# A decoder block whose feed-forward products are shared: the seven products of a saved multiplication kept in the accumulators' banks and multiplied one unit earlier, with landing tiles of half the size

## The chip, the cores and the metric

The kernel runs on one NeuronCore of a Trainium2 chip. What is compared is the device time of one execution in microseconds. PE is the matrix engine (TensorE), PEld its weight loads, DVE the vector engine, ACT the scalar engine, POOL GpSimd and SP the engine that issues most transfers. SBUF is the on-chip memory that the engines work from; PSUM is the small memory that PE writes sums to, eight banks of 128 x 512 fp32 each.

## The reference

One layer on 256 tokens of width 2048, all in fp32:

```
h = h + 0.5 * swiglu(rms_norm(h), ffn1_w_gate, ffn1_w_up, ffn1_w_down)     # D_FF = 5632
n = rms_norm(h); P = n @ w_in                                             # 5376 columns
h = h + concat(retention(P), sliding_window_attention(P)) @ w_out
h = h + memory_cross_attention(rms_norm(h), rms_norm(mem))                # 256 memory tokens
h = h + 0.5 * swiglu(rms_norm(h), ffn2_w_gate, ffn2_w_up, ffn2_w_down)
out = rms_norm(h)

swiglu(x, g, u, d) = (silu(x @ g) * (x @ u)) @ d
```

The two feed-forward networks (FFN 1 and FFN 2) hold about two thirds of the time. The change is in them.

## The kernel before

**Three matmuls for one.** PE multiplies in a rounded fp32 (fp32r). Each factor is split into a high part (ACT copies it, rounded) and a low part (DVE subtracts the high part), and `three` issues high x high, high x low and low x high into the same sum. A split of a weight piece of 128 x 1024 takes one ACT instruction (tile `wh`) and one DVE instruction (tile `wl`); both tiles have four buffers.

**Units and steps.** The products with weights are written as a list of units. A `Unit` is one block of 512 output columns for all 256 tokens; t = 0, 1 are the two halves of the tokens, and each has its own PSUM bank. A unit goes through blocks of 512 rows of the weight, each in two steps of 256 rows: a step is 2 token halves x 2 row blocks of 128 x 3 = 12 matmuls of 128 x 512. `run_stream` walks over all steps; before it writes step *at* it writes the splits up to step at + 3 (LOOKAHEAD) and the loads up to at + 8. What finishes a block, or moves it, hangs on a list of tasks: `later(d, f)` runs f when d steps more have been written. Loads land in tiles named `wf`, 1 MB each, five of them, issued on SP's queue.

**Twins.** In the FFNs two blocks of output columns f = 0, 1 (gate and up of one block, or two blocks of the down product) go together as a `Twin`. Of its four blocks of 512 rows three are plain steps: 3 x 2 x 2 = 12 of them. The fourth (`seven`) is a 2 x 2 by 2 x 2 block product (token halves x row halves, row halves x f) done with seven products in place of eight, in Winograd's form. A product is a step of 6 matmuls. Some products take sums of the left factor (`sums`, from `sums_of`: four ACT copies, four DVE additions, and a split on both engines) and differences of the weights (DVE, line 222). Before, four of the seven products go to banks of their own (`tmp`), DVE adds them into SBUF tiles (`first_sums`, `second_sums`) while the plain steps add up in the two `acc` tiles, and `parts` adds the two at the end of the Twin: 8 DVE additions of 128 x 512 and one ACT copy for each Twin. The products are written behind plain steps 2 to 8 of their own Twin.

An FFN is: gate and up of block 0 as two Units, Twins for blocks 1 to 3, two Twins of the down product, Twins for 4 to 7, two Twins down, Twins for 8 to 10, four Units down. I number the Twins of one FFN T0 to T13. `gate_done` (Silu on ACT) and `up_done` (DVE) take a finished pair, `cross` transposes it (DVE), writes it to DRAM (SP) and reads it back (POOL).

## Time and profile before

| | us |
|---|---|
| median of 3 runs (2145.35 to 2149.93) | 2148.33 |
| the profiled execution | 2148.38 |
| its span on the core | 2146.2 |
| PE busy in it | 2129.7 |
| DVE busy | 1664.5 |
| ACT busy | 1144.4 |

The profiled execution's own time is 2.2 us over its span, and 0.05 us from the median. FFN 1 lies between about 5 and 730 us of the span, the mixer and the cross attention up to about 1440 us, and FFN 2 behind that. In the tables of groups one row is the instructions of one line with the same tiles and shape: busy time, mean ns of one, and the time that the engine stood idle just before them. In rows in order of time the first number is the start in us, the second the duration. A matmul's duration runs to its modelled end; the next one starts earlier than that.

### The profile page before, as it was taken

What the parts mean: (1) busy time and instruction counts of PE and PEld (TensorE: products, weight loads), DVE (VectorE), ACT (ScalarE), POOL (GpSimd) and SP (SyncE); (2) the same over time, 40 slices, a digit from 0 to 9 for tenths busy, and PEclk for the clock granted to TensorE, in tenths of its full rate; (3) what the DMA queues carried; (4) which work ended last, traced back from release to release, by engine and by line L of the source; (5) the groups of instructions that cost most, each with busy time, mean ns of one, the idle gap of its engine ahead of it and who ended that gap; (6) DMA issues with size and microseconds to landing.
All of it is one profiled execution on the core that took longest, in us unless ns stands there. A gap on an engine that the chain in (4) does not pass through costs nothing.

```text
span 2146.2 us, 25612 instructions
## 1 busy us (share of the span) xinstructions
PE 2129.7 (99%) x9624; PEld 1764.9 (82%) x9624; DVE 1664.5 (78%) x1984; ACT 1144.4 (53%) x1395; POOL 159.1 (7%) x273
## 2 busy tenths in 40 slices
PE   9999999999999999999999999999999999999998
PEld 7888888888888878888788888888888888888886
DVE  6988888888885778787665555567988888888875
ACT  6555555555554554646455444455655455555554
POOL 0000100001001110101110110010100000000000
PEclk9999999999999999999999999999999999999999
DMA  7767676767657666666776766476876575656663
GB/s 295 238 205 253 233 239 224 246 218 253 230 202 255 216 225 207 204 208 221 251 249 214 241 218 206 156 245 235 250 269 225 178 249 203 233 200 228 205 227 141
DMA packets 138444, 482.50 MB, mean 225 GB/s; under 512 B 11984, under 2 KB 11984, under 8 KB 138192
## 3 DMA queue, kind: packets, MB, share of 16 engines
q1 hardware_dynamic: 125888, 447.26, 59.7%
q0 software_dynamic: 12288, 33.57, 6.7%
q8 instruction: 75, 1.23, 0.2%
q14 instruction: 49, 0.40, 0.1%
q10 hardware_dynamic: 144, 0.05, 0.0%
HBM read 445.17 MB, written 35.65 MB: 224 GB/s over the span
## 4 chain that ended last, share of the span: by engine, by line
PE 57%; DVE 2%; DMA 2%; issue 1%; ACT 0%; POOL 0%; POOLq 0%; ACTq 0%; DVEq 0%
PE acc L633 17%; PE acc L632 17%; PE acc L634 17%; DMA t4k<-box 2%; PE tmp L634 2%; PE tmp L632 2%; PE tmp L633 2%; DVE wl L79 1%; DVE h L647 0%; PE tmp L866 0%; POOL t4k L619 0%; DVE t4k L610 0%; PE tmp L847 0%; DVE blk L520 0%; DMA box<-t4k 0%
## 5 line engine op out<-in xcount | busy, mean ns | idle before, releaser
L74 ACT ACTIVATE wh<-wf 128x1024 fp32r<-128x1024 f32 (+1 forms) x861 | 905.9, 1056 | 884.5 <-PE acc L634 819.5
L79 DVE TENSOR_TENSOR wl<-wf,wh 128x1024 fp32r<-128x1024 f32 (+1 forms) x861 | 1037.9, 1215 | 373.4 <-ACT wh L74 357.6
L632 PE MATMUL acc<-wh,blk 128*128 128x512 f32 (+1 forms) x2832 | 1100.6, 389 | 1.2 <-ACT wh L74 1.2
L633 PE MATMUL acc<-wl,blk 128*128 128x512 f32 (+1 forms) x2832 | 1099.1, 388 | 1.1 <-DVE wl L79 1.0
L634 PE MATMUL acc<-wh,blk 128*128 128x512 f32 (+1 forms) x2832 | 1098.1, 388 | 0.0
L632 PEld LDWEIGHTS acc<-wh,blk 128*128 128x128 f32 x2832 | 533.0, 188 | 112.2 <-ACT wh L74 2.4
L633 PEld LDWEIGHTS acc<-wl,blk 128*128 128x128 f32 x2832 | 533.0, 188 | 109.0 <-DVE wl L79 1.9
L634 PEld LDWEIGHTS acc<-wh,blk 128*128 128x128 f32 x2832 | 532.9, 188 | 108.7
L619 POOL DMA_DIRECT2D t4k<-box x256 | 147.8, 584 | 1772.3 <-DMA box<-t4k 748.4
L222 DVE TENSOR_TENSOR wf<-wf,wf 128x1024 f32<-128x1024 f32 x84 | 102.6, 1222 | 1.9
L632 PE MATMUL tmp<-wh,blk 128*128 128x512 f32 x224 | 87.1, 389 | 0.0
L633 PE MATMUL tmp<-wl,blk 128*128 128x512 f32 x224 | 87.1, 389 | 0.0
L634 PE MATMUL tmp<-wh,blk 128*128 128x512 f32 x224 | 87.1, 389 | 0.0
L249 DVE TENSOR_TENSOR t2k<-t2k,acc 128x512 f32<-128x512 f32 x112 | 71.8, 683 | 9.5 <-PE acc L634 9.5
L249 DVE TENSOR_TENSOR t2k<-t2k,tmp 128x512 f32<-128x512 f32 x112 | 76.5, 684 | 1.9
L610 DVE STREAM_TRANSPOSE t4k<-t2k 128x512 f32<-128x512 f32 x96 | 63.0, 691 | 10.2 <-ACT t2k L74 10.0
L634 PEld LDWEIGHTS tmp<-wh,blk 128*128 128x128 f32 x224 | 42.0, 188 | 8.7
L632 PEld LDWEIGHTS tmp<-wh,blk 128*128 128x128 f32 x224 | 42.0, 188 | 8.7
L633 PEld LDWEIGHTS tmp<-wl,blk 128*128 128x128 f32 x224 | 42.0, 188 | 8.7
L79 DVE TENSOR_TENSOR blk<-t4k,blk 128x512 fp32r<-128x512 f32 (+2 forms) x72 | 44.1, 653 | 4.8 <-ACT blk L74 4.6
L74 ACT ACTIVATE blk<-t4k 128x512 fp32r<-128x512 f32 (+2 forms) x72 | 39.2, 596 | 7.5 <-DMA t4k<-box 7.5
L647 DVE TENSOR_TENSOR h<-h,t4k 128x512 f32<-128x512 f32 x40 | 25.8, 687 | 16.6 <-DMA t4k<-box 16.6
(149 smaller groups left out, 720.1 us busy)
## 6 DMA issues: line engine op xcount, KB each, us to landing
wf<-in_ffn_w_up SPq DMA_DIRECT2D x88, 1024.0 KB, 6.6
wf<-in_ffn_w_down SPq DMA_DIRECT2D x88, 1024.0 KB, 6.9
wf<-in_ffn_w_gate SPq DMA_DIRECT2D x87, 1024.0 KB, 6.9
box<-t4k SPq DMA_DIRECT2D x64, 512.0 KB, 3.3
t4k<-box POOLq DMA_DIRECT2D x256, 128.0 KB, 7.0
wf<-in_w_in_rqk SPq DMA_DIRECT2D x16, 1024.0 KB, 7.4
wf<-in_w_in_rvg SPq DMA_DIRECT2D x16, 1024.0 KB, 5.4
wf<-in_w_out SPq DMA_DIRECT2D x16, 1024.0 KB, 8.0
```

Of the source, the lines that this page charges most:

```text
L74: return nc.scalar.activation(dst, src, AF.Copy, **kw)
L79: nc.vector.tensor_tensor(lo, src, hi, ALU.subtract)
L222: nc.vector.tensor_tensor(src, p, q, ALU.subtract)
L249: nc.vector.tensor_tensor(out, a, b, ALU.add)
L610: nc.vector.transpose(z[:, t, :].rearrange("p (g q j) -> p q g j", g=4, q=4), squares_of(v))
L619: nc.gpsimd.dma_start(z[32 * g : 32 * g + 32].rearrange("p t (i n) -> p (t i) n", i=4), far[g])
L632: nc.tensor.matmul(o, ah, bh, start=start, stop=False)
L633: nc.tensor.matmul(o, ah, bl, start=False, stop=False)
L634: nc.tensor.matmul(o, al, bh, start=False, stop=stop)
L647: nc.vector.tensor_tensor(v, v, out[t], ALU.add)
```

## The change

1. The seven products accumulate in the four banks that hold the Twin's result. The banks are named (f, t). P1 goes to (0,0), P5 to (1,1), P6 to (0,1), P3 to (1,0). After P6 DVE adds the copy of P1 onto bank (0,1) there (`middle`), and P7 is accumulated on top of it. After P7 ACT copies bank (0,1), and DVE adds this copy to bank (1,1) and another sum to (1,0) (`spread`). P2 and P4 and the plain steps are accumulated behind that, and the finished sums are read from PSUM. For each Twin this is 4 ACT copies and 4 DVE additions.
2. All Twins but the first of each FFN are `ahead`: P1, P5, P6, P3, P7 stand between the plain steps of the preceding Twin, P7 behind its last one; P2 and P4 stand between their own plain steps. T0 has P1, P5, P6, P3, P2, P7 one after the other ahead of its first plain step.
3. For that two Twins' banks are open at once. Every other Twin (T0, T2, ... `spare`) takes four `tmp` tiles of one bank, the others the two `acc` tiles of two banks.
4. Landing tiles are 128 x 1024 (512 KB), ten of them. A load of a paired weight takes half of both column blocks: 256 runs of 2 KB, before 256 runs of 4 KB. The other loads have runs of 4 KB as before, 128 of them.

The matmuls are the same in number, shape and line of `three`, and outside the FFNs they stand in the same order.

```diff
-    def big(dt=F32):
-        return wpool.tile([P, 2, 1024], dt, tag="wf", name=nm("wf"), bufs=5)
+    def land(dt=F32):
+        return wpool.tile([P, 1024], dt, tag="wf", name=nm("wf"), bufs=LAND)
...
+        plan = {
+            P1: ((0, 0), (0, 0), (0, 0)),
+            P5: ((1, 0), (1, 1), 0),
+            P6: ((1, 0), (0, 1), 1),
+            P7: ((0, 0), (0, 1), 2),
+            P2: ((0, 1), (0, 0), (1, 0)),
+            P4: ((0, 1), (0, 1), (1, 1)),
+            P3: ((1, 1), (1, 0), 3),
+        }
...
+        def bank(self, f, t):
+            if self.spare:
+                if (f, t) not in self.acc:
+                    self.acc[f, t] = tmp_ps()
+                return self.acc[f, t]
+            if f not in self.acc:
+                self.acc[f] = ps_acc.tile([P, 2, 512], F32, tag="acc", name=nm("acc"))
+            return self.acc[f][:, t, :]
...
+            if last and kind in (P1, P5, P6, P7):
+                later(0, {P1: self.keep, P5: self.keep_other, P6: self.middle, P7: self.spread}[kind])
...
-        def first_sums(self):
-            self.u2 = self.add(t2k(), self.u1, self.products[5])
-            self.u3 = self.add(t2k(), self.u2, self.products[4])
-            self.u5 = self.add(t2k(), self.u3, self.products[3])
-
-        def second_sums(self):
-            self.u4 = self.add(self.u2, self.u2, self.products[3])
-
-        def parts(self, f):
-            xs = (self.u4, self.u5) if f else (self.u1, self.u3)
-            return [self.add(x, x, self.acc[f][:, t, :]) for t, x in enumerate(xs)]
+        def middle(self):
+            x = self.bank(0, 1)
+            self.add(x, self.u1, x)
+            self.u2 = self.copied(x)
+            self.add(self.p5, self.p5, self.u2)
+
+        def spread(self):
+            for x, y in ((self.copied(self.bank(0, 1)), self.bank(1, 1)), (self.p5, self.bank(1, 0))):
+                self.add(y, x, y)
...
+            if isinstance(u, Twin):
+                if not u.ahead:
+                    out += u.chunks((P1, P5, P6, P3, P2, P7))
+                chunks = u.chunks((P2, P4) if u.ahead else (P4,))
+            own, n = len(chunks), len(x)
+            if isinstance(after, Twin) and after.ahead:
+                chunks += after.chunks((P1, P5, P6, P3, P7))
+            space = len(chunks) if len(chunks) > own else 2 * own
+            for at, step in enumerate(x):
+                out.append(step)
+                for i, c in enumerate(chunks):
+                    place = (2 * i + 1) * n // (2 * space)
+                    if i < own:
+                        place = min(place, n - 4)
+                    if place == at:
+                        out.append(c)
...
+        twins.append(Twin(*args, ahead=bool(twins), spare=len(twins) % 2 == 0))
```

The order of the instructions changes at two kinds of places that matter below. The first is the start of T0, here in FFN 1. On PE, before, the last matmuls of the block-0 unit (`acc_220`) are followed by T0's first plain step (`acc_530`):

```order
L633 MATMUL acc_220<-wl_431,blk_399 128x512
L634 MATMUL acc_220<-wh_430,blk_399 128x512
L632 MATMUL acc_530<-wh_450,blk_135 128x512 [waits PE_49,Activation_49]
L633 MATMUL acc_530<-wl_451,blk_135 128x512
L634 MATMUL acc_530<-wh_450,blk_135 128x512
```

Now the unit is followed by P1 (`tmp_557`, here its end) and P5 (`tmp_570`), whose left factor `blk_554` is the split of the sums:

```order
L643 MATMUL tmp_557<-wl_464,blk_414 128x512
L643 MATMUL tmp_557<-wh_463,blk_414 128x512
L643 MATMUL tmp_570<-wh_489,blk_554 128x512 [waits Activation_49]
L643 MATMUL tmp_570<-wl_490,blk_554 128x512 [waits DVE_49]
L643 MATMUL tmp_570<-wh_489,blk_554 128x512 [waits DVE_49]
```

P5, the first product that takes sums, now stands 6 matmuls behind the unit's end; before, 72 matmuls (five plain steps and two products without sums) stood in between. On DVE, before, the same place reads so (`t2k_489` and `t2k_490` are the finished block, `blk_519` the sums, `blk_564` their low part):

```order
L695 SCALAR_TENSOR_TENSOR t2k_489<-acc_220,n_102,t2k_489 128x512 [waits PE_49,Pool_49]
L695 SCALAR_TENSOR_TENSOR t2k_490<-acc_220,n_102,t2k_490 128x512
L610 STREAM_TRANSPOSE t4k_515<-t2k_489 128x4x4x32 [waits DVE_49]
L610 STREAM_TRANSPOSE t4k_515<-t2k_490 128x4x4x32 [waits DVE_49]
L79 TENSOR_TENSOR wl_525<-wf_448,wh_524 128x1024 [waits DMAHW0_49,Activation_49]
L279 TENSOR_TENSOR blk_519<-blk_519 128x256 x2
L279 TENSOR_TENSOR blk_519<-blk_519 128x256 [waits DVE_49]
L79 TENSOR_TENSOR wl_549<-wf_493,wh_548 128x1024 [waits Activation_49]
L279 TENSOR_TENSOR blk_519<-blk_519 128x256 [waits DVE_49]
L79 TENSOR_TENSOR wl_572<-wf_448,wh_571 128x1024 [waits Activation_49]
L222 TENSOR_TENSOR wf_448<-wf_495,wf_448 128x2x2x256 [waits DMAHW2_49]
L79 TENSOR_TENSOR blk_564<-blk_519,blk_564 128x1024 [waits Activation_49]
```

and now (`blk_534` the sums, `blk_554` their low part):

```order
L696 SCALAR_TENSOR_TENSOR t2k_505<-acc_235,n_102,t2k_505 128x512 [waits PE_49,Pool_49]
L696 SCALAR_TENSOR_TENSOR t2k_506<-acc_235,n_102,t2k_506 128x512
L617 STREAM_TRANSPOSE t4k_530<-t2k_505 128x4x4x32 [waits DVE_49]
L617 STREAM_TRANSPOSE t4k_530<-t2k_506 128x4x4x32 [waits DVE_49]
L82 TENSOR_TENSOR wl_540<-wf_509,wh_539 128x1024 [waits Activation_49]
L291 TENSOR_TENSOR blk_534<-blk_534 128x256 x2
L291 TENSOR_TENSOR blk_534<-blk_534 128x256 [waits DVE_49]
L82 TENSOR_TENSOR wl_567<-wf_543,wh_566 128x1024 [waits DMAHW1_49,Activation_49]
L291 TENSOR_TENSOR blk_534<-blk_534 128x256 [waits DVE_49]
L236 TENSOR_TENSOR wf_543<-wf_543,wf_486 128x2x2x256 [waits DVE_49]
L82 TENSOR_TENSOR blk_554<-blk_534,blk_554 128x1024 [waits Activation_49]
L82 TENSOR_TENSOR wl_581<-wf_461,wh_580 128x1024 [waits PE_49,Activation_49]
```

The row is nearly the same; one split has gone from between the sums and their low part, and PE stands at a product of the sums where it stood at a plain step.

The second place is the hand-over from one Twin to the next on PE, here T4 to T5 of FFN 1. Before, T4's last matmuls (`acc_1870`) are followed by T5's first plain step into its own tile:

```order
L633 MATMUL acc_1870<-wl_2074,blk_1672 128x512
L634 MATMUL acc_1870<-wh_2073,blk_1672 128x512
L632 MATMUL acc_2159<-wh_2084,blk_135 128x512 [waits DVE_49,Activation_49]
L633 MATMUL acc_2159<-wl_2085,blk_135 128x512
L634 MATMUL acc_2159<-wh_2084,blk_135 128x512
```

Now T5's P7 (left factor `blk_554`) ends T4's unit, and T5's first plain step (`blk_150`) follows it into the same tile of two banks:

```order
L643 MATMUL acc_2107<-wh_2245,blk_554 128x512 [waits Activation_49]
L643 MATMUL acc_2107<-wl_2246,blk_554 128x512 [waits DVE_49]
L643 MATMUL acc_2107<-wh_2245,blk_554 128x512 x2
L643 MATMUL acc_2107<-wl_2246,blk_554 128x512
L643 MATMUL acc_2107<-wh_2245,blk_554 128x512
L643 MATMUL acc_2107<-wh_2257,blk_150 128x512 [waits Activation_49]
L643 MATMUL acc_2107<-wl_2258,blk_150 128x512 [waits DVE_49]
L643 MATMUL acc_2107<-wh_2257,blk_150 128x512 x2
L643 MATMUL acc_2107<-wl_2258,blk_150 128x512
```

The plain step starts with bank (0,0). Bank (0,1), which `spread` copies, is written by the plain step's second six matmuls; none of those carries a wait on ACT, and the step's first matmul does: there the wait for the copy stands, since both banks are one tile. Where the next Twin has `tmp` tiles of one bank each, the wait for the copy stands at the seventh matmul.

## The prediction

> **What bounds the kernel now.** First the page (shares of the engines), then the stretches of time in which the change works, then who waits for whom, then the rows in order of time at the two places where the order changes.

> ```profile
> span 2146.2 us, 25612 instructions
> PE 2129.7 (99%) x9624; PEld 1764.9 (82%) x9624; DVE 1664.5 (78%) x1984; ACT 1144.4 (53%) x1395; POOL 159.1 (7%) x273
> 65.00:700.00 635.00, 635.00 (x2803) 525.82 (x2802) 536.69 (x565) 347.20 (x368) 46.05 (x80) 1.00 0.69 232
> 1500.00:2130.00 630.00, 630.00 (x2780) 521.50 (x2779) 529.11 (x553) 336.78 (x356) 32.25 (x56) 1.00 0.65 220
> ```

> The first two lines are the page. The other two are stretches of the FFNs: length, then the busy time of PE, PEld, DVE, ACT, POOL, the granted clock, and the DMA share. PE is busy in 635.00 of 635.00 and in 630.00 of 630.00 us, at full clock. In the FFNs there is no wait that could be taken away, and any wait that is added is paid in full.

> ```profile
> 49.10 0.39 PE L632 MATMUL acc<-wh,blk 128*128 128x512 f32 x1
> ...
> 51.82 0.39 PE L632 MATMUL acc<-wh,blk 128*128 128x512 f32 x1
> ACT wh L74 <- PE acc L634: 819.5, 598, 5.6
> L249 DVE TENSOR_TENSOR t2k<-t2k,tmp 128x512 f32<-128x512 f32 x112 | 76.5, 684 | 1.9
> L74 ACT ACTIVATE t2k<-tmp 128x512 f32<-128x512 f32 x32 | 18.5, 579 | 0.0
> L74 ACT ACTIVATE wh<-wf 128x1024 fp32r<-128x1024 f32 x852 | 901.1, 1061 | 882.4 <-PE acc L634 819.5 <-PE tmp L634 31.8 <-issue 9.2
> ```

> From 49.10 to 51.82 PE does the twelve matmuls of one step: 2.72 us, 0.227 each, so a product of 6 takes 1.36. ACT waits 819.5 us for PE (a buffer for `wh` comes free). A DVE addition takes 0.68 us, a copy out of PSUM 0.58, a high part 1.06.

> **What costs nothing.** The matmuls are the same; PE's work stays. Twenty-eight Twins lose 4 additions each: 112 x 0.684 = 77 us of DVE, off the path, since PE is busy in all of both stretches. They gain 3 copies each: 84 x 0.579 = 49 us of ACT, against 819.5 us in which ACT waits for PE; if that cover were gone, all of it would be paid. Where products stand between plain steps, `middle` has four of these, 10.9 us, until P7 needs its bank, for an addition and a copy.

> ```profile
> wf<-in_ffn_w_up SPq DMA_DIRECT2D x88, 1024.0 KB, 6.6
> box<-t4k SPq DMA_DIRECT2D x64, 512.0 KB, 3.3
> 2.60 0.52 SPq L333 DMA_DIRECT2D wf<-in_ffn_w_up  x1
> ```

> Landing: 1024 KB in runs of 4 KB take 6.6 us, 512 KB in runs of 2 KB (the write of `box`) 3.3: the same for a byte, and the DMA share has room from 0.69. SP issues 863 transfers (counted in the new order) in place of 476, at about half a microsecond each some 430 us of the span, in order; a `box` write waits on SP behind fewer outstanding bytes than before. Ten half tiles less the four that a Twin holds leave the loads some six steps, over 13 us, ahead: nothing. If transfers came late, DVE's and ACT's splits would be the first to wait.

> **Term 1: the start of T0.** P5 and P6 and P3 need the sums 1.36 us after the block-0 unit ends. ACT's and DVE's rows of FFN 1, before:

> ```profile
> 46.45 0.16 DVE L570 TENSOR_SCALAR ms<-tmp 128x2 f32<-128x2 f32 x1 [0.70 <-PE tmp L568]
> 49.36 1.27 ACT L674 ACTIVATE t2k<-acc,n 128x512 f32<-128x512 f32 x2 [2.49 <-PE acc L634]
> 51.61 1.23 DVE L79 TENSOR_TENSOR wl<-wf,wh 128x1024 fp32r<-128x1024 f32 x1 [3.48 <-ACT wh L74]
> 52.75 1.40 DVE L695 SCALAR_TENSOR_TENSOR t2k<-acc,n,t2k 128x512 f32<-128x512 f32 x2
> ...
> 58.53 0.42 DVE L279 TENSOR_TENSOR blk<-blk 128x256 f32<-128x256 f32 x1
> 58.86 1.22 DVE L79 TENSOR_TENSOR wl<-wf,wh 128x1024 fp32r<-128x1024 f32 x1
> 60.00 1.22 DVE L222 TENSOR_TENSOR wf<-wf,wf 128x1024 f32<-128x1024 f32 x1
> 61.13 1.23 DVE L79 TENSOR_TENSOR blk<-blk,blk 128x1024 fp32r<-128x1024 f32 x1
> ```

> The finished block (L695) to the fourth sum takes 52.75 to 58.86, 6.11 us, for ten instructions that stand in the new order too: the sums wait behind the finished block, its transposes and two splits. Then comes one subtraction (1.14 from start to start) and the low part (1.23), beside which ACT makes the high part. The chain begins a little later: from 46.61 on, DVE and ACT take turns for P5 and P6 (subtraction 1.14, high part 1.06, low part 1.14, subtraction 1.14, high part 1.06, low part 1.14) and are done at 53.4, not 52.75. So the low part is there at 53.4 + 6.11 + 1.14 + 1.23 = 61.9. P1 ends at 51.82 + 1.36 = 53.18; two matmuls of P5 need only the high part. PE loses 61.9 - 53.18 - 0.45 = 8.3 us. Later P7 waits for ACT's copy, which stands behind two high parts: 0.3.

> ```profile
> 1482.15 1.41 DVE L695 SCALAR_TENSOR_TENSOR t2k<-acc,n,t2k 128x512 f32<-128x512 f32 x2 [0.70 <-PE acc L634]
> ...
> 1487.93 0.42 DVE L279 TENSOR_TENSOR blk<-blk 128x256 f32<-128x256 f32 x1
> ...
> 1490.54 1.22 DVE L79 TENSOR_TENSOR blk<-blk,blk 128x1024 fp32r<-128x1024 f32 x1
> ```

> In FFN 2 the block's end was waited for until 1482.15, so PE's next matmul could start at about 1481.95 and P1 would end at 1483.3. L695 to the fourth sum is 6.12 us (1482.15 to 1488.27), now with 0.35 ahead of it (the rest of a subtraction), and behind it a split, a subtraction and the low part: 1482.5 + 6.12 + 1.14 + 1.14 + 1.22 = 1492.1. Meanwhile five matmuls can go. Loss: 1492.1 - 1483.3 - 1.13 = 7.7. Then P7's copy stands behind three high parts: 1.2.

> ```profile
> 1043.99 0.39 PE L632 MATMUL acc<-wh,blk 128*128 128x512 f32 x1
> 1045.93 0.62 PE L568 MATMUL tmp<-ones,t2k 128*128 128x1 f32 x4 [1.55 <-DVE t2k L565]
> 1046.42 0.78 PE L633 MATMUL acc<-wl,blk 128*128 128x512 f32 x1
> ...
> 1049.90 0.40 PE L632 MATMUL acc<-wh,blk 128*128 128x512 f32 x1
> 1040.00:1060.00 20.00, 18.45 (x77) 14.92 (x76) 11.95 (x15) 7.83 (x9) 3.03 (x5) 0.91 0.81 259
> ```

> A pause has a price behind it. After 1.9 us without work the eight matmuls from 1046.42 to 1049.90 took 3.48 us in place of 1.81, and the granted clock of the stretch is 0.91: 1.7 us lost. T0's pause is longer, so I take 1.6 each; none is the least, twice that the most. Term 1: 8.3 + 0.3 + 1.6 = 10.2 and 7.7 + 1.2 + 1.6 = 10.5, together 20.7 (14 to 26).

> **Term 2: the hand-over.** Before, no such wait stood there, so its price is put together:

> ```profile
> 1269.39 0.39 PE L634 MATMUL acc<-wh,blk 128*128 128x512 f32 x1
> 1269.82 0.69 ACT L74 ACTIVATE blk<-acc,nmem 128x512 fp32r<-128x512 f32 x1 [1.61 <-PE acc L634]
> 7.23 0.63 ACT L74 ACTIVATE wh<-wf 128x512 fp32r<-128x512 f32 x1 [1.28 <-DMA wf<-in_ffn_w_gate]
> 7.45 0.28 PE L634 MATMUL acc<-wh,blk 128*128 128x256 f32 x1
> 7.91 0.38 PE L632 MATMUL acc<-wh,blk 128*128 128x256 f32 x1 [0.18 <-ACT wh L74]
> ```

> ACT starts 0.43 us after the start of the last matmul that it waits for; the copy takes 0.58; PE starts 0.05 after ACT's end (7.86, 7.91), and the matmul after a wait takes 0.10 longer (0.38, 0.28). 0.43 + 0.58 + 0.05 + 0.10 less the usual 0.23 is 0.93 us. It is paid where the next Twin has the two-bank tiles: T1, T3, ..., T13, seven in each FFN. At the other hand-overs six matmuls, 1.36 us, lie between P7 and the wait, against 0.83: nothing. In FFN 1 the finished blocks of T4 and T10 are scaled by ACT, so a copy (to 1.01 after the unit's last matmul), a high part (to 2.07) and then the copy (to 2.65) precede: PE goes on at 2.70 where it would at 1.59, 1.21 with the 0.10. Term 2: 12 x 0.93 + 2 x 1.21 = 13.6 (8 if only the copy's 0.58 counts, 17 at 1.21 each).

> **Sum**, against the profiled execution's 2148.38 (0.05 from the median): 2148.4 + 20.7 + 13.6 = 2182.7, so 2183. Bounds of the terms: 2148.4 + 22 = 2170 and 2148.4 + 43 = 2191.

> **Rivals.**
> *The hand-over is free.* If only the bank that ACT reads were kept from PE, bank (0,0)'s six matmuls would cover it: 2148.4 + 20.7 = 2169. Against: the order has the wait at the first of them. [...]
> *T0's sums are early.* ACT's and DVE's queues may have the sums ahead of the finished block after all, if the 3.48 us in which DVE stands idle ahead of it (row at 51.61) are used for them; then T0 costs little: 2148.4 + 13.6 = 2162. Against: the sums stand behind L695 in the order, and that waits for PE.
> *PE passes a waiting matmul.* Behind P5 and behind each hand-over stand matmuls that wait for nothing. If PE went on with these, both terms would vanish, and 2148.4 is left, with a few us either way from waits outside the FFNs such as that at 1043.99: 2145 to 2150, not slower. It decides if PE passes at all. Against: at 1043.99 PE stood 1.9 us at a matmul that waited for DVE, with plain matmuls right behind it. [...]
> *ACT is late everywhere.* If a high part of 1.06 us precedes the copy at all 26 hand-overs, the twelve others cost about half a microsecond each and the fourteen 0.3 to 1.1 more: about 2197.

> **Chances.** Forecast 0.68; free hand-over 0.10; early sums 0.07; PE passes 0.05; ACT late 0.10. The range 2161 to 2193 takes in the first three and leaves out 0.15. A measurement of this kernel tells about 0.2% (4 us) from no change. PE passing is shared between faster and the same, with 0.01 of the rest for each of them: faster 0.03, same 0.04, slower 0.93.

> **What would show it.** PE's busy time in 65 to 700 us falls short of the stretch by about 8 us, at about 0.9 for each wait of `acc` for ACT's t2k copy, every second Twin. At 53 and at 1483 us PE stands 6 to 7 us for `blk`, and the granted clock behind it drops. DVE is busy some 75 us less, ACT 50 us more. I am wrong if PE stands at other places, above all if splits wait for `wf`, or if T0's waits are under 4 us.

## The result: 1.75% slower, as forecast

The changed kernel takes 2185.15 us (median of 4 runs, 2182.87 to 2187.39), the kernel before 2147.27 beside it: ratio 1.0175, 95% interval 1.0158 to 1.0193. The prediction was 2183. The profiled execution took 2185.12 us, its span is 2183.3.

The page of the changed kernel, and the two stretches of the FFNs (length, then PE, PEld, DVE, ACT, POOL, granted clock, DMA share):

```profile
span 2183.3 us, 26696 instructions
PE 2141.8 (98%) x9624; PEld 1767.3 (81%) x9624; DVE 1592.0 (73%) x1872; ACT 1180.0 (54%) x1479; POOL 159.2 (7%) x273
65.00:700.00 635.00, 629.94 (x2764) 518.47 (x2763) 489.38 (x494) 355.92 (x398) 43.75 (x76) 1.00 0.71 229
1500.00:2130.00 630.00, 617.90 (x2702) 507.58 (x2701) 485.59 (x492) 350.02 (x387) 34.58 (x60) 0.99 0.68 221
```

PE's matmuls are as many as before, DVE is busy 72 us less, and PE no longer fills its stretches: it misses 5.1 us in the first and 12.1 in the second, which holds T0's stop of FFN 2 (1502 to 1509) while T0 of FFN 1 lies ahead of the first. Its waits say where (us in all, times, longest; the last row is the kernel before):

```profile
PE tmp L643 <- ACT blk L77: 14.4, 2, 7.8
PE acc L643 <- ACT t2k L77: 9.8, 14, 0.8
PE tmp L575 <- DVE t2k L572: 5.0, 2, 4.1
PE tmp L568 <- DVE t2k L565: 4.3, 3, 1.8
```

The first row is T0's wait for the sums, twice; the second is the hand-over, fourteen times; the third is two waits for norms, 4.1 us of it for that of FFN 2, which was not in the prediction.

A wait's price is more than the wait (in FFN 1 T0's wait of 7.78 us for the sums stands in a stretch that grew by 11.1), so the time is also counted from start to start. All kernels run the same 9624 matmuls; numbered by their start in the trace, the time between the starts of two numbers is what that stretch of work took. In us:

```
matmuls        0-234   234-320  320-2900  2900-6500  6500-6732  6732-6830  6830-9400
               start   T0 FFN1  rest FFN1  middle     norm FFN2  T0 FFN2    rest FFN2
before          50.5    19.5     584.8      772.4      53.4       22.2       582.5
changed         51.5    30.6     592.2      766.5      59.0       33.1       589.6
changed again   50.7    30.9     592.2      770.5      58.5       33.1       589.6
e1 sums early   51.1    26.5     592.2      765.6      54.3       29.9       589.6
e2 one bank     51.2    30.1     584.8      764.6      59.9       32.5       582.5
e3 both         51.6    26.7     587.0      765.3      57.2       25.5       584.1
e4 half tiles   50.5    19.5     584.9      769.6      53.9       22.2       582.5
e5 norm first   50.9    31.0     592.2      765.8      52.3       33.5       589.6
e7 no subtr.    50.7    22.7     592.2      767.6      58.8       24.2       589.6
e8 copy twice   50.5    30.9     596.8      766.4      54.6       33.1       593.6
e6 T0 spread    55.7    21.6     585.3      765.7      54.5       23.7       582.5
e9 again        50.4    28.2     584.8      764.7      52.3       22.4       582.5
e10 norm later  50.5    28.2     584.8      764.6      53.6       23.1       582.5
e11 T0 mended   53.4    23.4     584.8      765.9      52.4       22.4       582.5
```

(In e6, e9, e10 and e11 some of T0's products stand among the matmuls numbered before T0's column, so there the two columns belong together.) The tail is 50.5 to 50.7 in all. Changed less before: 1.0, 11.1, 7.4, -5.9, 5.6, 10.9 and 7.1, together 37.2 us. So T0 cost 22.0, the hand-overs 14.5, and two things outside the prediction, +5.6 at the norm of FFN 2 and -5.9 in the middle, cancelled in this execution; in a second profile of the same kernel the middle gave only 1.9.

T0 of FFN 1, in order of time:

```profile
53.99 0.39 PE L643 MATMUL tmp<-wh,blk 128*128 128x512 f32 x1
54.81 1.40 DVE L696 SCALAR_TENSOR_TENSOR t2k<-acc,n,t2k 128x512 f32<-128x512 f32 x2
...
60.59 0.42 DVE L291 TENSOR_TENSOR blk<-blk 128x256 f32<-128x256 f32 x1
60.93 1.22 DVE L236 TENSOR_TENSOR wf<-wf,wf 128x1024 f32<-128x1024 f32 x1
61.05 1.06 ACT L77 ACTIVATE blk<-blk 128x1024 fp32r<-128x1024 f32 x1 [3.92 <-DVE blk L291]
...
62.13 1.22 DVE L82 TENSOR_TENSOR blk<-blk,blk 128x1024 fp32r<-128x1024 f32 x1
...
62.16 0.79 PE L643 MATMUL tmp<-wh,blk 128*128 128x512 f32 x1 [7.78 <-ACT blk L77]
...
63.41 1.22 PE L643 MATMUL tmp<-wh,blk 128*128 128x512 f32 x2
...
50.00:70.00 20.00, 12.18 (x43) 9.05 (x42) 16.10 (x19) 10.67 (x15) 2.47 (x4) 0.74 0.58 160
```

PE's matmul at 53.99 is the last of P1. The finished block (L696) comes first on DVE, the fourth sum (L291) at 60.59, ACT's high part of the sums behind that, and PE goes on at 62.16, 8.17 us later in place of 0.23. The low part (L82) is done at 63.35, and P5's third matmul, the first that needs it, starts at 63.41. The granted clock of these 20 us is 0.74: of the matmuls behind the stop eight start 0.43 us apart. In FFN 2 the like stop ends at 1509.26, 6.96 us behind P1's last matmul. At a hand-over into two-bank tiles:

```profile
112.74 0.39 PE L643 MATMUL acc<-wh,blk 128*128 128x512 f32 x1
113.16 0.60 ACT L77 ACTIVATE t2k<-acc 128x512 f32<-128x512 f32 x1 [0.30 <-PE acc L643]
...
113.81 0.50 PE L643 MATMUL acc<-wh,blk 128*128 128x512 f32 x1 [0.69 <-ACT t2k L77]
...
114.15 0.40 PE L643 MATMUL acc<-wl,blk 128*128 128x512 f32 x1
```

From 112.74 to 113.81 are 1.07 us, and 0.34 to the next, where 0.227 is usual: 0.96 us lost.

### The profile page after: what moved, and what is told of

Read it like the earlier page. It is cut to its first block, busy times and chain, and to the rows that moved or that the text cites. A ratio compares the mean times of both kernels' runs of the same rounds, so it can differ in the third digit from the quotient of the medians.

```text
span 2183.3 us, 26696 instructions
## 1 busy us (share of the span) xinstructions
PE 2141.8 (98%) x9624; PEld 1767.3 (81%) x9624; DVE 1592.0 (73%) x1872; ACT 1180.0 (54%) x1479; POOL 159.2 (7%) x273
## 3 DMA queue, kind: packets, MB, share of 16 engines
q8 instruction: 75, 1.23, 0.2%
## 4 chain that ended last, share of the span: by engine, by line
PE 60%; DVE 1%; DMA 1%; ACT 1%; issue 0%; ACTq 0%; POOLq 0%; POOL 0%; DVEq 0%; SPq 0%
PE acc L643 44%; PE tmp L643 15%; DMA wf<-in_ffn_w_up 1%; DVE wl L82 0%; PE tmp L873 0%; ACT t2k L77 0%; PE tmp L854 0%; PE tmp L947 0%; PE tmp L820 0%; ACT wh L77 0%; PE tmp L575 0%; PE tmp L969 0%; PE tmp L966 0%; PE tmp L968 0%; PE tmp L948 0%
## 5 line engine op out<-in xcount | busy, mean ns | idle before, releaser
L643 PE MATMUL acc<-wh,blk 128*128 128x512 f32 (+1 forms) x4376 | 1371.1, 389 | 10.8 <-ACT t2k L77 9.8
L82 DVE TENSOR_TENSOR wl<-wf,wh 128x1024 fp32r<-128x1024 f32 (+1 forms) x861 | 1035.9, 1215 | 460.8 <-ACT wh L77 453.9
L643 PEld LDWEIGHTS acc<-wh,blk 128*128 128x128 f32 x4376 | 820.9, 188 | 185.9 <-ACT t2k L77 15.7
L643 PE MATMUL acc<-wl,blk 128*128 128x512 f32 (+1 forms) x2188 | 849.0, 388 | 0.7 <-DVE wl L82 0.7
L643 PE MATMUL tmp<-wh,blk 128*128 128x512 f32 x1736 | 558.8, 392 | 14.8 <-ACT blk L77 14.4
L643 PEld LDWEIGHTS acc<-wl,blk 128*128 128x128 f32 x2188 | 412.3, 188 | 83.1 <-DVE wl L82 1.5
L643 PEld LDWEIGHTS tmp<-wh,blk 128*128 128x128 f32 x1736 | 327.9, 189 | 86.4 <-ACT blk L77 15.2
L643 PE MATMUL tmp<-wl,blk 128*128 128x512 f32 x868 | 339.8, 391 | 0.4 <-DVE wl L82 0.4
L643 PEld LDWEIGHTS tmp<-wl,blk 128*128 128x128 f32 x868 | 164.1, 189 | 35.2 <-DVE wl L82 1.2
L236 DVE TENSOR_TENSOR wf<-wf,wf 128x1024 f32<-128x1024 f32 x112 | 136.8, 1222 | 35.4 <-DMA wf<-in_ffn_w_up 23.4
L77 ACT ACTIVATE t2k<-acc 128x512 f32<-128x512 f32 x72 | 42.2, 598 | 31.9 <-PE acc L643 22.6
L77 ACT ACTIVATE t2k<-tmp 128x512 f32<-128x512 f32 x68 | 40.5, 596 | 28.8 <-PE tmp L643 21.9
L82 DVE TENSOR_TENSOR blk<-t4k,blk 128x512 fp32r<-128x512 f32 (+2 forms) x72 | 44.1, 652 | 4.1 <-ACT blk L77 3.9
## 6 DMA issues: line engine op xcount, KB each, us to landing
wf<-in_ffn_w_gate SPq DMA_DIRECT2D x176, 512.0 KB, 7.3
wf<-in_ffn_w_up SPq DMA_DIRECT2D x176, 512.0 KB, 7.8
wf<-in_ffn_w_down SPq DMA_DIRECT2D x176, 512.0 KB, 7.7
box<-t4k SPq DMA_DIRECT2D x64, 512.0 KB, 3.3
wf<-in_w_in_rqk SPq DMA_DIRECT2D x32, 512.0 KB, 8.8
wf<-in_w_in_rvg SPq DMA_DIRECT2D x32, 512.0 KB, 7.3
wf<-in_w_out SPq DMA_DIRECT2D x32, 512.0 KB, 7.9
```

Source lines behind the costliest of these rows:

```text
L77: return nc.scalar.activation(dst, src, AF.Copy, **kw)
L82: nc.vector.tensor_tensor(lo, src, hi, ALU.subtract)
L236: nc.vector.tensor_tensor(dst, p, q, ALU.subtract)
L643: nc.tensor.matmul(o, x, y, start=first, stop=last, skip_group_check=shared)
```

## The experiments

Each was timed beside the kernel before; ratios are to that.

**Is the hand-over the two-bank tile's?** e2: the accumulators' tiles get one bank each (four of them, in Twins and other units); the order of PE's matmuls in the Twins stays.

```diff
-                self.acc[f] = ps_acc.tile([P, 2, 512], F32, tag="acc", name=nm("acc"))
-            return self.acc[f][:, t, :]
+            if (f, t) not in self.acc:
+                self.acc[f, t] = tmp_ps() if self.spare else acc_bank()
+            return self.acc[f, t]
...
+        return ps_acc.tile([P, 512], F32, tag="acc", name=nm("acc"))
```

> The two-bank tiles of the accumulators become one-bank tiles, four of them; the order of the matmuls stays, but at the hand-over the wait for ACT's copy now stands at the seventh matmul behind P7 instead of the first. Theory (PE waits because the tile has two banks, and the copy takes 0.85 us beyond the normal interval at 14 places, with 0.11 behind it): 2185.1 - 14 x 0.97 = 2171.5, say 2169 to 2174, and the 1.08 us gaps are gone. Rival (PSUM or ACT itself is what is slow, whichever tile it is): 2184 to 2186. Rival (ACT's copy comes late at most places, over 1.36 us behind P7): the gaps only shrink, 2175 to 2180.

2166.21 us (2162.3 to 2174.26), ratio 1.0086 (1.0067 to 1.0105): 3 us under the theory's range, with runs that spread over 12 us. In the profiled one (2168.18) the stretches behind T0 give 14.5 us back and the middle 1.9. Behind T0 they are at 584.8 and 582.5, to the tenth those of the kernel before. The first such hand-over in e2:

```profile
112.36 0.60 ACT L77 ACTIVATE t2k<-acc 128x512 f32<-128x512 f32 x1 [0.29 <-PE acc L651]
112.38 0.39 PE L651 MATMUL acc<-wl,blk 128*128 128x512 f32 x1
...
112.61 0.62 PE L651 MATMUL acc<-wh,blk 128*128 128x512 f32 x2
```

ACT copies one bank (0.60 us) while PE writes another at its full pace, its matmuls 0.22 to 0.23 us apart. So what the prediction's rival by bank took for granted holds here; what two engines in one bank would do, no run shows. The rival didn't come true because the wait in the order was for a tile, not for a bank.

e8 doubles the suspected cost: the copy behind P7 is made twice.

```diff
         def spread(self):
+            self.copied(self.bank(0, 1))
             for x, y in ((self.copied(self.bank(0, 1)), self.bank(1, 1)), (self.p5, self.bank(1, 0))):
```

> The changed kernel with each Twin's copy behind P7 made twice, the second into a buffer of its own that nobody reads. Theory (the copy lies on PE's path at the 14 hand-overs into two-bank tiles and is covered by six matmuls, 1.36 us, at the others): 14 x 0.58 = 8.1 us more, 2193, the gaps there 1.65 us in place of 1.08; where the tiles have one bank 0.83 + 0.58 = 1.41 against 1.36, 0.1 us or less each. Rival (the hand-over was never paid by the copy's length, but by some fixed cost of a wait): 2185 to 2187.

2193.0 us (2188.49 to 2198.12), ratio 1.0215 (1.0197 to 1.0233).

```profile
PE acc L644 <- ACT t2k L77: 16.6, 14, 1.2
...
112.46 1.09 ACT L77 ACTIVATE t2k<-acc 128x512 f32<-128x512 f32 x2 [0.30 <-PE acc L644]
...
113.60 0.50 PE L644 MATMUL acc<-wh,blk 128*128 128x512 f32 x1 [1.18 <-ACT t2k L77]
```

Two copies take 1.09, 0.49 more than one, and the fourteen waits grow from 9.8 to 16.6 us, 0.49 each. The stretches grow by 4.6 and 4.0: 6.8 at these fourteen, the rest at the hand-overs into one-bank tiles, some 0.1 us each as expected and 0.5 at one. Taken away and doubled, the copy moves the time by its own length: the hand-over is shown.

**Is T0's stop the late sums?** e1 makes the sums earlier, in FFN 1 three steps, in FFN 2 right behind the norm.

```diff
-            if b == 0:
-                sums_of(norm, 3, sums, 1)
...
+        if norm is n1:
+            later(13, lambda: sums_of(norm, 3, sums, 0))
+        else:
+            st["early"] = lambda: sums_of(norm, 3, sums, 0)
```

(`st["early"]` is called five steps behind the last block of the cross attention's output.)

> The sums for T0 are made about three steps earlier in FFN 1 and right behind the norm in FFN 2, so that they are ready when P5 comes; all else is as in the changed kernel (2185.1 us). Theory (the late sums make T0's stop): the two stops of 8.17 and 6.96 us go, and with them the slow matmuls behind them (about 12 each at 0.43 instead of 0.227, 2.4 us): 2185.1 - 7.9 - 6.7 - 4.8 = 2165.7, say 2163 to 2169; no PE gap over 2 us is left at 53 and 1502 us. Rival (the stop is the chain of subtraction and high part on DVE and ACT, or the landing of the weights, and the sums only stand beside it): most of the stop stays, 2175 to 2185. A second risk: the sums, now ahead of the splits, make PE wait a step earlier, some 2 us each.

2177.71 us (2171.66 to 2179.39), ratio 1.0138 (1.0119 to 1.0156): 7.4 us less in the medians, where 19 were expected, and in the range of the rival. The two stops of 8.17 and 6.96 us are gone, but the stretches of T0 shrank only from 30.6 to 26.5 and from 33.1 to 29.9. What stands there now, in FFN 1:

```profile
54.30 2.48 DVE L236 TENSOR_TENSOR wf<-wf,wf 128x1024 f32<-128x1024 f32 x2
...
55.61 2.01 ACT L77 ACTIVATE wh<-wf 128x1024 fp32r<-128x1024 f32 x2 [2.49 <-DVE wf L236]
...
56.72 0.49 PE L643 MATMUL tmp<-wh,blk 128*128 128x512 f32 x1 [1.09 <-ACT wh L77]
...
60.38 3.46 DVE L82 TENSOR_TENSOR wl<-wf,wh 128x1024 fp32r<-128x1024 f32 x3
...
61.62 0.51 PE L643 MATMUL tmp<-wl,blk 128*128 128x512 f32 x1 [0.59 <-DVE wl L82]
...
65.13 0.50 PE L643 MATMUL tmp<-wh,blk 128*128 128x512 f32 x1 [0.69 <-ACT t2k L77]
```

PE waits in turn for a high part behind two subtractions, for a low part, and at P7 for ACT's copy. In FFN 2 two stops of 2.18 and 2.05 us follow each other, for a high part and for a low part, where no gap over 2 us was to be left. PE does a product in 1.36 us; one with a subtraction keeps DVE busy for 2.4 (1.22 + 1.23). Back to back, T0's six products ask more of DVE (six low parts and three subtractions, 11.0 us) and of ACT (six high parts and four copies, 8.7 us) than of PE (8.2 us), an estimate from the durations of single rows (1.22, 1.05, 0.60 and 1.36). The expectation missed that the sums hid a second chain of nearly their length.

e7 takes the subtractions out of that chain, on top of e1.

```diff
-            if kind in (P5, P6, P7, P4):
+            if kind in (P5, P6, P7, P4) and self.ahead:
```

> The kernel with the early sums, and T0 (of both FFNs) without its subtractions of weights: it multiplies by the plain weights, so those two Twins compute something else; every other instruction stays. Theory (with the sums there, T0 is bound by DVE and ACT, and DVE's subtractions, 1.14 us each, stand in the chain to P5, P6 and P7): the stops of 1.49, 0.95 and 0.59 us behind P1 in FFN 1 and their like in FFN 2 shrink by 2 to 3.5 us in each FFN, 4 to 7 us in all; the waits of P7 and of the hand-over for ACT's copies (1.09 and 1.27 us) stay. Rival (ACT's high parts and copies alone set the pace): no change within 2 us.

2168.31 us (2165.81 to 2169.43), ratio 1.0098 (1.0084 to 1.0111). T0 takes 22.7 and 24.2: 3.8 and 5.7 less than in e1, more than the 4 to 7 expected for both, with the slow matmuls behind the stops going too (in FFN 1 they start 0.43 us apart from 58.26 us on in e1, 0.23 behind e7's stops). What is left, 3.2 and 2.0 us, is mostly two waits for ACT's copies and one for a low part. So of T0's 22.0 us, taken away in this order, 7.3 went with the late sums, 9.5 with the subtractions behind them, and 5.2 stayed.

e3 has the edits of e1 and e2 together.

> Both edits together. Theory (two separate terms, nothing else slower in the FFNs): 2185.1 - 19.4 - 13.6 = 2152.1, range 2147 to 2156, that is some 5 us above the kernel before, by the longer wait for the norm of FFN 2 (4.4 us in the changed kernel, 1.35 before, with slow matmuls behind it) and T0's short stops at P6 and P7 (about 1 us in each FFN). Rival (ACT or DVE or the landings become the next limit once the stops no longer give them slack): 2157 to 2170.

2157.91 us (2154.24 to 2161.8), ratio 1.0042 (1.0027 to 1.0058): above the theory's range, at the low end of the rival's. T0 keeps 7.2 and 3.3 us, by the chain of e7, the norm keeps 3.8, and each FFN has a new stop of 1.6 us further on (2.2 and 1.6 in the stretches), at 555 and 1556 us. There PE waits for a low part, as the rival had it; why the low part is late there was not followed up.

**The landing tiles alone.** e4 is the kernel before, its Twins and their order, with the changed kernel's `land` and `load` (one place of several):

```diff
-            loaded[at], loaded[other] = load_pair(self.w[f], b) if self.pair else load(self.w[f], 2 * b, 2)
+                out, self.other[b, which] = (load(self.w[which], 2 * b + i) for i in range(2))
```

> The kernel before with the landing tiles of the changed kernel (ten of 512 KB in runs of 2 KB, each with a transfer of its own) and without its new products: they stay in banks of their own, and stand in the Twin's own steps. Theory of the prediction (nothing): 2147.3, within 2 us, and the wait for the norm of FFN 2 as before, 1.35 us. Rival (the landings, 7.3 to 7.8 us for half the bytes in the changed kernel against 6.6 to 6.9, hold something up, the norm of FFN 2 above all): 2150 to 2154, and that wait 3 to 5 us.

2145.33 us (2141.62 to 2150.25), ratio 0.9984 (0.9974 to 0.9994). Half tiles cost nothing; what they bring lies in the middle, where PE stood 1.14 us at the norm of the cross attention in place of 1.94, without the slow matmuls behind it (0.23 us apart, 0.43 in the kernel before). They are neither the 37 us nor the norm of FFN 2 (53.9 us; its wait is 1.84). The middle is shorter in every trace with half tiles (764.6 to 770.5 us, before 772.4), because at its two norms the turned block lands earlier against PE's work (0.3 to 1.6 us at the first, 0.8 to 2.8 at the second but in e12). Whether the half tiles do that isn't shown: there is one trace of the kernel before.

**The norm of FFN 2.** This place of the changed kernel, and the same in e5, which moves one DVE instruction, the subtraction for P5 of T0 (L236), behind the norm:

```profile
1470.35 1.29 DVE L658 TENSOR_TENSOR h<-h,t4k 128x512 f32<-128x512 f32 x2 [3.92 <-DMA t4k<-box]
...
1478.07 1.23 DVE L236 TENSOR_TENSOR wf<-wf,wf 128x1024 f32<-128x1024 f32 x1 [1.17 <-DMA wf<-in_ffn_w_up]
1479.21 2.35 DVE L82 TENSOR_TENSOR wl<-wf,wh 128x1024 fp32r<-128x1024 f32 x2
1481.48 0.42 DVE L572 TENSOR_TENSOR t2k<-t2k 128x256 f32<-128x256 f32 x1
...
1481.95 1.01 PE L575 MATMUL tmp<-ones,t2k 128*128 128x1 f32 x4 [4.05 <-DVE t2k L572]
```

```profile
1467.45 1.29 DVE L662 TENSOR_TENSOR h<-h,t4k 128x512 f32<-128x512 f32 x2 [1.90 <-DMA t4k<-box]
...
1476.40 0.42 DVE L574 TENSOR_TENSOR t2k<-t2k 128x256 f32<-128x256 f32 x1
...
1476.87 0.61 PE L577 MATMUL tmp<-ones,t2k 128*128 128x1 f32 x4
...
1477.59 1.23 DVE L236 TENSOR_TENSOR wf<-wf,wf 128x1024 f32<-128x1024 f32 x1
```

```diff
+                if not self.ahead and "finish" in st:
+                    order(st["finish"], nc.cur_bb.bb.instructions[-1])
```

> The changed kernel with one DVE instruction moved: the subtraction for P5 of T0 of FFN 2, which stood ahead of the last addition of the norm of FFN 2 and waited 1.17 us for its weights, now stands behind that norm. Theory (this subtraction, 1.17 + 1.23 us, is why PE waits 4.4 us for the norm where it waited 1.35 before): PE's wait at 1477 us shrinks from 4.44 to about 2.0, with fewer slow matmuls behind it, 2 to 4 us in all: 2181 to 2183. Rival (the block itself comes late, by the landing of its turned box, 11.5 us from the read's issue against 10.4 before): the wait stays above 4 us, 2184 to 2186.

2177.92 us (2176.21 to 2184.04), ratio 1.0153 (1.0136 to 1.017): a larger gain than either theory or rival expected, but that interval overlaps the changed kernel's, so the gain isn't settled by the times. In the trace PE's wait is gone altogether, where 2.0 us were expected. The kernel before:

```profile
1456.00 1.29 DVE L647 TENSOR_TENSOR h<-h,t4k 128x512 f32<-128x512 f32 x2 [3.22 <-DMA t4k<-box]
...
1464.74 0.42 DVE L565 TENSOR_TENSOR t2k<-t2k 128x256 f32<-128x256 f32 x1
```

From the block's addition to the norm's are 11.13 us in the changed kernel, 8.95 in e5 and 8.74 before: the subtraction's share is 2.2. The rest is when the block lands: in e5 it landed 2.0 us earlier against PE's work, so not all of e5's gain is its edit's. A second profile of the changed kernel, e12, was to show that part:

> The changed kernel once more, unaltered, for a second trace of its waits. Theory (the wait for the norm of FFN 2 has two parts, the subtraction ahead of it, 2.4 us in every run, and the landing of the turned block, which differs from run to run): 2183 to 2187; the wait is 2.3 to 4.7 us, not under 2, and the T0 stops and the hand-overs are as before within 0.1 us. Rival (the norm's wait is all of one cause): 4.3 to 4.6 us again.

2185.47 us (2184.53 to 2188.19), ratio 1.0178 (1.0157 to 1.0198); the wait for the norm is 4.03 us from start to start, the chain from block to norm 10.91. In e8, where this place has the same order, the chain is 11.71 and the wait 2.54, since the block landed earlier against PE's work. The two parts add up in every trace. Counted from the start of matmul 6500, PE's last matmul ahead of the norm starts at 35.36 us. The block's addition starts at the time in the first column, the norm's last addition one chain later, and PE goes on 0.47 us behind the start of that:

```
                block  chain  PE's wait, start to start
before          27.50   8.74  1.35
changed         28.20  11.13  4.44
changed again   28.02  10.91  4.03
e8 copy twice   25.71  11.71  2.54
e5 norm first   26.18   8.95  none
e7 no subtr.    29.83   8.73  3.67
```

In e7, whose T0 has no subtraction, the chain is as short as before, and the wait comes of the late block alone. So the chain is the order's and the rest the landing's, which differs by 4 us between these traces; with the chain of before the changed kernel would still have waited 2.0 us. The wait in the middle differs as well: none at the norm of the cross attention in the first profile, 2.75 us in this one.

**Towards a better version.** e6 is e3 with e5's edit and T0's products between the preceding unit's last steps; e9, e10 and e11 mend what its trace showed.

```diff
+                        p1, p5, p6, p3, p2, p7 = first
+                        out = out[:-6] + [p1] + out[-6:-3] + [p5, out[-3], p6, out[-2], p3, out[-1], p2, p7]
```

> Both edits of the earlier run (sums early, one-bank tiles), the subtraction behind the norm, and T0's products put between the last plain steps of the unit ahead: P1, P5, P6 and P3 in FFN 2, only P1 and P5 in FFN 1, where the tokens' last block comes too late for more. Theory (what is left of T0 is a chain of subtractions, splits and copies that DVE and ACT do more slowly than PE does the products; with plain steps between them it is covered): from the 2157.9 of both edits, 3.3 us less in FFN 2, about 3 in FFN 1, 2.5 at the norm: 2149, range 2146 to 2153, no stop over 1 us left at T0 of FFN 2. Rival (the landings set T0's pace, since seven products ask for four half tiles at once): T0 stays within 2 us of what it was, 2154 to 2158.

2151.34 us (2147.78 to 2153.39), ratio 1.0019 (1.001 to 1.0028), in the theory's range. T0 falls to 21.6 and 23.7, though in FFN 2 one stop of 1.52 us stays, for ACT's copy at the hand-over, where none over 1 us was expected. But in FFN 1 the sums now stood ahead of the norm on DVE:

```profile
44.64 0.75 DVE L303 TENSOR_TENSOR blk<-blk 128x256 f32<-128x256 f32 x2
...
48.93 0.42 DVE L588 TENSOR_TENSOR t2k<-t2k 128x256 f32<-128x256 f32 x1
...
49.40 0.61 PE L591 MATMUL tmp<-ones,t2k 128*128 128x1 f32 x4 [3.26 <-DVE t2k L588]
```

e9, in FFN 1 and in FFN 2 (e6, then e9):

```diff
-            later(12, lambda: sums_of(norm, 3, sums, 0))
+            later(13, lambda: sums_of(norm, 3, sums, 0))
...
-                        out = out[:14] + first[:1] + out[14:15] + first[1:2] + out[15:] + first[2:]
+                        out = out[:15] + first[:1] + out[15:] + first[1:]
...
-                        out = out[:-6] + [p1] + out[-6:-3] + [p5, out[-3], p6, out[-2], p3, out[-1], p2, p7]
+                        out = out[:-6] + [p1] + out[-6:-3] + [p5, out[-3], p6, out[-2], p3, out[-1], p7, p2]
```

> As the kernel with T0's products spread (2151.3 us), with three places mended: in FFN 1 the sums start one step later again, so that they no longer stand ahead of the norm (PE waited 3.65 us for it), and only P1 goes between plain steps; in FFN 2 P2 stands behind P7, so that twelve matmuls (2.7 us) cover the copy at the hand-over, where 1.52 us was left. Theory: 3.4 us and some slow matmuls less at the norm, 2 to 3 more at T0 of FFN 1 (P5 and P6 back to back again), 1.3 less at T0 of FFN 2: 2151.3 - 5 + 2.5 - 1.3 = 2147.5, range 2144 to 2151, level with the kernel before (2145.8 in the last runs). Rival (T0 of FFN 1 costs its 7 us again): 2151 to 2154.

2149.09 us (2147.0 to 2154.49), ratio 1.0016 (1.0007 to 1.0025). That is in the theory's range, but T0 of FFN 1 did what the rival said: back to back again, it costs 8.7. In FFN 2 the norm and T0 cost nothing any more, the norm because its block landed 3.6 us earlier than in e6.

e10 is e9 with one change:

```diff
-    n2 = Norm(G_FFN2, "n2", 4)
+    n2 = Norm(G_FFN2, "n2", 5)
```

> The same, with the norm of FFN 2 one step later in the order of PE and DVE. Theory (PE waited 2.47 us for it since the additions on DVE come late; one step of plain matmuls, 2.7 us, covers that, and one more split on DVE takes 1.2 of it back): 1.2 to 2.4 us less, with the slow matmuls behind the wait 2 to 3: 2145, range 2142 to 2148, so at best 0.1% under the kernel before and more likely no different. Rival (T0's sums, now with the norm in the same step, come late for P5): 2146 to 2149.

2148.86 us (2147.68 to 2155.27), ratio 1.0019 (1.001 to 1.0028): outside the theory's range and no gain, since e9 had no wait for that norm left. Two new stops of about 1 us, for a low part and a high part, took its place.

e11 has e6's order in FFN 1 and e9's in FFN 2, and:

```diff
-            later(13, lambda: sums_of(norm, 3, sums, 0))
+            later(12, lambda: sums_of(norm, 3, sums, 0, (0, 2, 2.5)))
```

(The last argument: how many steps later the scaling, the additions and the split come.)

> As the kernel with T0's products spread again (2149.1 us), and T0 of FFN 1 mended: its sums are made in three pieces around the norm (scaling one step before it, additions and split right behind it), so that P1 and P5 can both stand between the last plain steps. Theory (T0 of FFN 1 is all that is left of the change's cost: 28.2 us there against 19.5, of which the kernel with P1 and P5 between plain steps had 21.6): 6 us less, 2143, range 2141 to 2147, 0.1 to 0.2% under the kernel before. Rival (PE waits for the norm instead, 3.65 us as in the first of these kernels): 2147 to 2150.

2148.1 us (2145.55 to 2152.87), ratio 1.0 (0.9987 to 1.0013): above the expected range, though not by the rival's wait for the norm. T0 of FFN 1 costs 3.9, with stops of 2.28 and 1.24 us for ACT's copies, and 2.9 more stand ahead of it, where PE waits 1.58 us for a high part and slow matmuls follow. The kernel as a whole is as fast as before by a balance: these 6.8 us against 6.5 less in the middle and 1.0 less at the norm of FFN 2, which the saved additions were not meant to bring. What the change itself is worth shows in the stretches behind T0. With its waits gone they take 584.8 and 582.5 us, to the tenth what they took before, though DVE does less work in them: DVE's 72 us were never on the path. The only version under the kernel before is e4, by 0.16%.

## Why the prediction was right

*What bounds the kernel.* Right: every microsecond lost is a stop of PE or the slow matmuls behind one, and no gain came of DVE's saved additions.

*Term 1, T0, 20.7 us (14 to 26).* Measured 22.0, from parts that differ more than the sum does. The low part, put at 61.9, was done at 63.35: DVE's chain began at 54.81 and not at 53.4 (the working's own figures give 53.3), but P1 ended a microsecond late as well (54.2, put at 53.18). So the stop still lost about what was forecast, 7.9 us (8.3), and 6.7 in FFN 2 (7.7). The slow matmuls were undersized: 2.8 and 2.7 us, put at 1.6 each. The waits at P7 were 0.4 and 1.3, put at 0.3 and 1.2. That stops and slow matmuls err in opposite ways is luck. The step holds, but its reason is half the truth: "the sums wait behind the finished block" is what PE waits for, and e1 shows that without this wait two thirds of the loss stay, by subtractions and splits that the prediction counted only until the low part of the sums.

*Term 2, the hand-over, 13.6 us (8 to 17).* Twelve gaps lose 0.96 us each (0.93 forecast), those behind T4 and T10 of FFN 1 1.03 (1.21): 13.6, and 14.5 by the stretches. e2 and e8 show the mechanism; PE's busy time fell short of the stretch by less than the 8 us foretold, since a matmul counts 0.39 us as busy, beyond the 0.227 to the next.

*What costs nothing.* DVE had 72 us less (77 forecast) and ACT was busy 36 more (49 forecast), in time that it had waited before, as forecast. SP issued 861 transfers, 863 by the prediction's count. For the landing tiles "the same for a byte" is wrong as a row; the second row here is e4's:

```profile
wf<-in_ffn_w_up SPq DMA_DIRECT2D x176, 512.0 KB, 7.8
wf<-in_ffn_w_up SPq DMA_DIRECT2D x176, 512.0 KB, 5.7
DVE wf L236 <- DMA wf<-in_ffn_w_up: 23.4, 12, 4.1
DVE wf L236 <- DMA wf<-in_ffn_w_down: 10.5, 5, 3.1
```

Half a tile took 7.8 us to land in the changed kernel and 5.7 in e4, where a whole one took 6.6; why the same tile takes longer in the changed kernel was not followed up. DVE's subtractions waited 33.9 us for weights in all, where the trace of the kernel before has no such wait. The prediction had named splits that wait for `wf` as a sign of being wrong. "Nothing" holds all the same for the tiles alone (e4) and in the stretches behind T0, where PE stops for more than 0.1 us at the fourteen hand-overs alone, but one of those waits, 1.17 us, stood ahead of the norm of FFN 2.

*What the sum left out.* The step that failed is the queue of DVE at T0 of FFN 2: the prediction followed the moved subtraction to P5 but not past the norm that it now precedes. That cost 5.6 us together with a block that landed 0.7 us later and the slow matmuls behind the stop; the middle gave 5.9 back, as two blocks landed earlier, for a reason that is open. The two terms were 2.2 us short (36.5 measured, 34.3 forecast); that the whole came within 3 us of the measured 37.2 is luck as far as those two cancelled.

*The rivals.* PE passed no waiting matmul: at each of the fourteen hand-overs it stood some 0.7 us at the plain step's first matmul and took none of the five behind it, which carry no wait for ACT (in e2, with that wait away, they start at once, 0.23 us apart). At T0 there was nothing to pass to: all matmuls of P5, P6 and P3 need the sums, and P2 writes P1's bank, which ACT copied only from 62.01 on. ACT was late at no hand-over: the gaps are alike to 0.1 us. The sums were not early; made early in e1, they gave 7.4 us and not the 20.7 that the rival gave them.

## What to carry to other kernels

When a wait is taken away, ask what is late next on the same path: count the whole chain on each engine against what the waiting engine does in that time, not the first wait alone. Here the buffer's tile, not the bank it lies in, set the wait that the framework put in (14.5 us over the hand-overs, none of it left in e2); before work is moved, make the tile as small as what is handed over. Follow a moved instruction down its own engine's queue to everything that now stands behind it, norms and other rare chains above all.

## What the runs showed of the hardware

```profile
735.80:739.20 3.40, 3.40 (x18) 3.40 (x17) 0.81 (x1) 0.00 (x0) 1.39 (x1) 0.50 0.75 295
1046.40:1049.80 3.40, 3.40 (x10) 2.73 (x10) 1.29 (x2) 0.00 (x0) 2.60 (x5) 0.50 1.01 366
```

In these traces the length of a stop doesn't decide alone. Stops of 1.58 (e11), 1.80 (e4), 1.94 and 2.07 (before) and 2.75 us (e12) were followed by one stretch of 3.41 us; stops of 1.84 (e4), 2.26 (e1), 2.28 (e11), 2.47 (e6) and 2.54 (e8) by none; every stop from 2.75 us up had at least one.
